# One attention block: TensorE, VectorE and ScalarE in the order of the source from the first head's steps to the last

## The chip, the cores and the metric

The kernel runs on one core of a Trainium2 chip. The metric is device time in microseconds (us) of one execution. Three runs of the kernel before took 638.62, 634.58 and 634.19 us: a median of 634.58 us. The profile comes from one more execution, which took 633.2 us.

## The reference

The kernel computes one residual block with two groups of attention heads that share one input projection. 16 learned rows stand ahead of the 1024 rows of `x`, so L = 1040.

```
h = RMSNorm(x);  proj = h @ w_in         # 1024 -> q, k, v, forget logits, gates, latents
8 FoX heads (width 64):  softmax(q k^T / 8 + sum of log f, causal) v
8 MLA heads (64 + 32 rotary): q and k, v from RMS-normed latents;
                         softmax(q k^T / sqrt(96), a key counts up to the end of the query's chunk of 64) v
y = concat(fox * silu(gate), mla * silu(gate)) @ w_out
out = x + RMSNorm(y), without the 16 learned rows
```

## The kernel before, in words

**Parts.** Operands of TensorE are held as a high and a low 16-bit part, so a product is three matmuls (high x high, high x low, low x high). Up to about 145 us the input is normalised and the first projections run. Then come 16 heads, 8 FoX and 8 MLA, and from about 575 us the output projection and the last norm.

**A step.** A head is four steps, and there are 64 of them. `step` (L891) takes a pair of 128-row query tiles, (7,0), (6,1), (5,2) or (4,3), so each step has 1184 columns of scores in all. In a step:

- `scores` (L798, and the mask as a matmul, L801) fill a PSUM tile `sc`. There are two such tiles, used in turn.
- `peaks` takes the two row maxima on VectorE (L808) and makes the bias `nbs` (L810).
- ScalarE takes two exponentials into `pr`: L905 for the short tile, L907 for the long one (elements in all: 1184 per row).
- `older_step` (L879) multiplies the weights of the step three before (LAG = 3) with the values (L834, L836, L837). Its result goes into the PSUM tile of the step *before this one*, and ScalarE copies it out (L889, `ona`). That copy frees the tile, and the next step's scores are written into that tile.
- `evacuate` empties a product's PSUM that is still owed on VectorE; `low` (L827, VectorE, twice) makes the low parts of the previous step's weights, GpSimd a small strip of them (L921), and SP issues one transposing DMA (L924) that brings them as `pT` to SBUF for the values' matmuls two steps later. `high` (L823) casts this step's weights on ScalarE.

**Jobs between the steps.** `run_head` calls `work` after each step. It issues pieces of what later heads need, each in a `product`, of which two PSUM buffers go round; product k+2 therefore waits until product k has been emptied. The jobs: the next FoX head's projection (L973 to L975, emptied by ScalarE L1060, L1061 and VectorE L1066, L1067); gates (tanh L1085, VectorE L1089 or L1092); MLA queries (weights split by L1179 on ScalarE and L1180 on VectorE, matmuls L1187 to L1189, VectorE L1193, split L144 and L147); MLA keys of two heads (L1205 to L1207 in three pieces, ScalarE L1210 twice and VectorE L1214 twice for each piece); early pieces of the output projection (L1272 to L1274, ScalarE L1291, a DMA to `y_d` L1292). After every second head `pair_end` transposes the outputs (L863, a product too), multiplies by the gate (L865) and splits. Squares of the output weights (L1128), their sum (L1136) and their splitting (L151) are put at given steps.

**What sets the order.** A scheduler places the instructions of every engine by priorities and a cost model of its own; it may hold one back or bring it ahead of what stands earlier in the source. Each engine then runs its list in that order. SP and GpSimd have their own lists.

Of the kernel before, what the change touches and what calls it, by code (L numbers as in the profile page):

```python
# [15 lines left out]
AF = mybir.ActivationFunctionType  # L16
# [32 lines left out]
def hybrid_kernel(ctx, tc, x, meta, norm_pre, norm_post, w_in, b_f, q_norm, w_uq, kv_norm, w_ukv, w_out,  # L49
# [3 lines left out]
    V, A, G, T, SY = nc.vector, nc.scalar, nc.gpsimd, nc.tensor, nc.sync  # L53

    def pool(name, bufs=1, space=None, side=None):
        kw = {}
        if space is not None:
            kw["space"] = space
        if side is not None:
            kw["side"] = side  # L60
        st = ExitStack()
        return st.enter_context(tc.tile_pool(name=name, bufs=bufs, **kw)), st
# [36 lines left out]
    def column(name):  # L99

        col[name] = t = const.tile([P, 1], F32, name=name)
        return t
# [64 lines left out]
    def mul(eng, name, a, b, c=None, op=ALU.mult):  # L167

        t = column(name)
        eng.tensor_scalar(t, a, b, c, ALU.mult, *(() if c is None else (op,)))  # L170
        return t
# [498 lines left out]
    def mla_factors():  # L670


        suk, isuk, suq, isuq, skr = (col[n] for n in ("suk", "isuk", "suq", "isuq", "skr"))
        sqm = mul(G, "sqm", suq, 0.5, CAP, ALU.min)
        skn = mul(G, "skn", suk, 0.125, CAP, ALU.min)
        smin = column("smin")
        G.tensor_scalar(smin, skn, skr, None, ALU.min)
        sm = mul(G, "sm", sqm, smin)
        cmk = mul(G, "cmk", skn, isuk, 1.0 / LATK)
        ism, iskn, iskr = (column(n) for n in ("ism", "iskn", "iskr"))  # L680
        for dst, src in ((ism, sm), (iskn, skn), (iskr, skr)):
            V.reciprocal(dst, src)
        rqs, rq0 = column("rqs"), mul(G, "rq0", sm, isuq, 1.0 / LATQ)
        G.tensor_scalar(rqs[0:64], rq0[0:64], iskn[0:64], None, ALU.mult)
        G.tensor_scalar(rqs[64:P], rq0[64:P], iskr[64:P], None, ALU.mult)
        gqs = const.tile([P, 2], F32, name="gqs")
        G.tensor_scalar(gqs, gq, suq, None, ALU.mult)
        gkvs = mul(G, "gkvs", gkv, suk)
        return ism, cmk, rqs, gqs, gkvs
# [9 lines left out]
    def step_psum(name):  # L699

        return ps_s.tile([P, 1536], F32, name=name, tag="sc")
# [61 lines left out]
    def evacuate():  # L763
        while evacs:
            evacs.popleft()()
# [6 lines left out]
    def product(name):  # L772
        evacuate()
        return ps_g.tile([P, 512], F32, name=name, tag="g")
# [8 lines left out]
    def places(ia, ib):  # L783

        wa, wb = NM + P * (ia + 1), NM + P * (ib + 1)
        a0 = AVW + (wb if (AVW + wa) % 512 < P else 0)
        b0 = AVW + (wa if a0 == AVW else 0)
        assert (a0 + wa - 1) % 512 >= P - 1 and (b0 + wb - 1) % 512 >= P - 1
        return (a0, wa), (b0, wb)

    def scores(i, passes, mask, mask_w, sc, c0, w):

        o = c0
        while o < c0 + w:
            o1 = min(c0 + w, (o // 512 + 1) * 512)
            last = o1 == c0 + w
            for q, (sta, mov) in enumerate(passes):
                T.matmul(sc[:, o:o1], sta[:, i * P : (i + 1) * P], mov[:, o - c0 : o1 - c0],  # L798
                         start=q == 0, stop=q == len(passes) - 1 and not last)
            o = o1  # L800
        T.matmul(sc[:, o - mask_w : o], ident16, mask, start=False, stop=True)  # L801
        return sc[:, c0:o]

    def peaks(parts, inv):

        nb = at.tile([P, 2], F32, name="nb", tag="nb", bufs=4)
        for k, part in enumerate(parts):
            V.tensor_reduce(nb[:, k : k + 1], part, AX.X, ALU.max, negate=True)  # L808
        nbs = at.tile([P, 2], F32, name="nbs", tag="nbs", bufs=4)
        V.tensor_scalar(nbs, nb, inv, LN_PSCALE, ALU.mult, ALU.add)  # L810
        return nbs[:, 0:1], nbs[:, 1:2]
# [6 lines left out]
    def high(i, pr, ph):  # L818
        W = NM + P * (i + 1)
        if i == 0:  # L820
            V.tensor_copy(ph[:, 112 : 112 + W], pr)
        else:
            A.copy(ph[:, 112 : 112 + W], pr)  # L823

    def low(i, pr, ph, lo):
        W = NM + P * (i + 1)
        V.tensor_tensor(lo, pr[:, NM:W], ph[:, P : P + W - NM], ALU.subtract)  # L827

    def weighted(av, i, hi, lo, vh):

        n = i + 1
        for j in range(n + 1):
            vl, v1 = Vt[:, j, vh, 0:HD], Vt[:, j, vh, HD : 2 * HD + 1]
            T.matmul(av, hi[:, j, :], v1, start=j == 0, stop=False)  # L834
            if j > 0:
                T.matmul(av, lo[:, j - 1, :], v1, start=False, stop=False)  # L836
            T.matmul(av[:, 0:HD], hi[:, j, :], vl, start=False, stop=j == n)  # L837
# [41 lines left out]
    def older_step(n, ps):  # L879

        old = steps.get(n - LAG)
        if old is None:
            return
        (ia, ib), pT = old["t"], old["pT"]
        vh, ona, after = old["rest"]
        av = ps[:, 0 : 2 * (HD + 1)].rearrange("p (i d) -> p i d", i=2)
        weighted(av[:, 1], ia, pT, pT[:, B0 + ib + 2 :, :], vh)
        weighted(av[:, 0], ib, pT[:, B0:, :], pT[:, ia + 2 :, :], vh)
        A.copy(ona[:, ib : ia + 1 : ia - ib, :], av)  # L889

    def step(first):  # L891

        now[0] += 1
        n = now[0]
        if first is not None:
            (ia, ib), passes, mask, mask_w, inv = first[0:5]
            last, psc[0] = psc[0], step_psum("sc")
            ps = psc[0]
            (a0, wa), (b0, wb) = places(ia, ib)
            sc = [scores(i, passes, mask, mask_w, ps, c0, w) for i, c0, w in ((ia, a0, wa), (ib, b0, wb))]  # L900
            nbs = peaks(sc, inv)
            pr = last_pr[0] = at.tile([P, wa + wb], F32, name="pr", tag="pr", bufs=2)
            prs = pr[:, 0:wa], pr[:, wa : wa + wb]

            A.activation(prs[1], sc[1], AF.Exp, bias=nbs[1], scale=inv)  # L905
            older_step(n, last)
            A.activation(prs[0], sc[0], AF.Exp, bias=nbs[0], scale=inv)  # L907
            ph = phs[n % NPH]
            la, lb = (B0 + ib + 2) * P, (ia + 2) * P
            los = ph[:, la : la + (ia + 1) * P], ph[:, lb : lb + (ib + 1) * P]  # L910
            steps[n] = dict(t=(ia, ib), pr=prs, prw=pr, ph=ph, phs=(ph, ph[:, B0 * P :]), los=los, rest=first[5:])
        else:
            older_step(n, product("av"))
        evacuate()
        prev = steps.get(n - 1)
        if prev is not None:
            for i, p, h, l in zip(prev["t"], prev["pr"], prev["phs"], prev["los"]):
                low(i, p, h, l)
            ph, n1 = prev["ph"].rearrange("p (b k) -> p b k", k=P), prev["prw"].rearrange("p (b k) -> p b k", k=NM)
            w0 = 1 + 8 * (prev["t"][0] + 1)  # L920
            G.tensor_tensor(ph[:, 0 : B0 + 1 : B0, 96:112], n1[:, 0 : w0 + 1 : w0, :],  # L921
                            ph[:, 0 : B0 + 1 : B0, 112:128], ALU.subtract)
            prev["pT"] = at.tile([P, NBLK * P], F16, name="pT", tag="pT", bufs=3).rearrange("p (b k) -> p b k", k=P)
            SY.dma_start_transpose(prev["pT"], prev["ph"])  # L924
        if first is not None:
            for i, p, h in zip((ia, ib), prs, steps[n]["phs"]):
                high(i, p, h)
        for fn in agenda.pop(n, ()):
            fn()
        old = steps.pop(n - LAG, None)  # L930
        if old is not None:
            (ia, ib), after = old["t"], old["rest"][-1]
            if after is not None:
                after(ia, ib)
# [283 lines left out]
        return [(0.8, gen(c0, n), None) for c0, n in CHUNKS]  # L1218

    ism, cmk, rqs, gqs, gkvs = mla_factors()  # L1220
    wkr = []

    def load_wk():
# [124 lines left out]
    for h in range(H):  # L1348
# [28 lines left out]
        last = (lambda o=onat, p=4 + p4: pair_end(o, p)) if hh else None  # L1377
        run_head(H + h, h, hh, ((QH, KH), (QL, KH), (QH, KL)), blk, 64, ism, onat, last, tiles_end if h == H - 1 else None)


    tl, tl_st = pool("tl", side="left")
    ctx.enter_context(tl_st)
# [66 lines left out]
    for t in order[:2]:  # L1449
        load_late(t)  # L1450
    step(None)
    A.activation(warm, last_pr[0][:, 0:1], AF.Sqrt)
    for t in order[:3]:
        load_rows(t)
    chains.popleft()()
    products(order[0], 0, 7)
    step(None)
    chains.popleft()()
    for k, t in enumerate(order):
# [50 lines left out]
```

## Time and profile before

| | |
|---|---|
| median of three runs | 634.58 us |
| the profiled execution | 633.2 us |
| its span, first to last instruction | 631.0 us |
| around the span | 2.2 us |
| TensorE busy | 559.9 us, 89% |
| VectorE busy | 455.5 us, 72% |
| ScalarE busy | 419.4 us, 66% |
| mean granted TensorE clock | 0.975 |

"Busy" counts time in which at least one instruction of the engine runs. An idle row of an engine matters only where the engine is late for something that sets the end. A granted clock of 1.00 is 2.4 GHz, of 0.50 is 1.2 GHz. Step n is counted from 0, head h has steps 4h to 4h+3; FoX heads are 0 to 7, MLA heads 8 to 15. By the starts of their scores the heads 0 to 14 take 31.2, 32.2, 31.6, 33.3, 30.0, 26.5, 34.7, 30.1 us (FoX) and 21.0, 22.4, 21.1, 25.2, 21.2, 26.7, 18.7 us (MLA).

### The profile page before, as it was taken

What the parts mean: (1) busy time and instruction counts of PE and PEld (TensorE: products, weight loads), DVE (VectorE), ACT (ScalarE), POOL (GpSimd) and SP (SyncE); (2) the same over time, 40 slices, a digit from 0 to 9 for tenths busy, and PEclk for the clock granted to TensorE, in tenths of its full rate; (3) what the DMA queues carried; (4) which work ended last, traced back from release to release, by engine and by line L of the source; (5) the groups of instructions that cost most, each with busy time, mean ns of one, the idle gap of its engine ahead of it and who ended that gap; (6) DMA issues with size and microseconds to landing.
All of it is one profiled execution on the core that took longest, in us unless ns stands there. A gap on an engine that the chain in (4) does not pass through costs nothing.

```text
span 631.0 us, 12856 instructions
## 1 busy us (share of the span) xinstructions
PE 559.9 (89%) x4914; PEld 339.2 (54%) x4914; DVE 455.5 (72%) x889; ACT 419.4 (66%) x756; POOL 197.5 (31%) x283
## 2 busy tenths in 40 slices
PE   2999799989898988999988897887989979989994
PEld 1445354546465655756666454554656656655442
DVE  3778876576767775767676667779777867777667
ACT  5788868456867776656657748578777767677322
POOL 2223333372224242324331322123322212331242
PEclk9999899999899999999999998999989989999998
DMA  8858768165687896696968588977978777698953
GB/s 286 213 133 222 152 175 211 33 179 162 123 179 144 195 192 120 123 194 141 166 127 177 100 199 175 192 148 131 167 168 163 142 156 160 129 189 191 302 180 120
DMA packets 269533, 105.11 MB, mean 167 GB/s; under 512 B 234832, under 2 KB 257360, under 8 KB 269472
## 3 DMA queue, kind: packets, MB, share of 16 engines
q1 hardware_dynamic: 269472, 104.30, 74.2%
q8 instruction: 38, 0.62, 0.4%
q14 instruction: 23, 0.19, 0.1%
HBM read 48.38 MB, written 13.96 MB: 99 GB/s over the span
## 4 chain that ended last, share of the span: by engine, by line
DVE 19%; PE 18%; ACT 12%; issue 7%; DMA 7%; SPq 2%; POOL 0%; DVEq 0%; ACTq 0%; POOLq 0%
DVE nb L808 7%; ACT pr L907 4%; DMA pT<-ph 4%; ACT ph L823 4%; DVE ph L827 3%; PE sc L798 2%; PE psf L1274 2%; PE psf L1272 2%; PE psf L1273 2%; DVE nbs L810 1%; DMA wqr<-in_w_uq 1%; SPq L924 1%; PE psg L973 1%; PE psg L975 1%; PE psg L974 1%
## 5 line engine op out<-in xcount | busy, mean ns | idle before, releaser
L827 DVE TENSOR_TENSOR ph<-pr,ph 128x512 f16<-128x512 f32 (+7 forms) x128 | 99.4, 782 | 67.7 <-ACT ph L823 66.7
L921 POOL TENSOR_TENSOR ph<-pr,ph 128x32 f16<-128x32 f32 x64 | 53.1, 830 | 228.1 <-ACT ph L823 106.7
L808 DVE TENSOR_REDUCE nb<-sc 128x1 f32<-128x1040 f32 (+7 forms) x128 | 93.2, 766 | 6.9 <-PE sc L801 6.3
L798 PE MATMUL sc<-st,st 128*128 128x256 f16 (+5 forms) x496 | 76.8, 293 | 8.5 <-ACT ona L889 7.3
L823 ACT CAST ph<-pr 128x784 f16<-128x784 f32 (+6 forms) x112 | 78.0, 740 | 0.2
L798 PEld LDWEIGHTS <-st 128*128 128x128 f16 x640 | 56.8, 99 | 37.5 <-issue 9.0
L834 PE MATMUL sc<-Vt,pT 128*128 128x65 f16 x671 | 64.7, 195 | 11.4 <-ACT pr L907 8.8
L837 PEld LDWEIGHTS <-pT 128*128 128x128 f16 x704 | 63.0, 99 | 11.6 <-issue 10.8
L837 PE MATMUL sc<-Vt,pT 128*128 128x64 f16 x671 | 66.5, 194 | 0.0
L834 PEld LDWEIGHTS <-pT 128*128 128x128 f16 x704 | 62.5, 98 | 7.2 <-DMA pT<-ph 4.8
L836 PE MATMUL sc<-Vt,pT 128*128 128x65 f16 x549 | 60.8, 195 | 0.0
L836 PEld LDWEIGHTS <-pT 128*128 128x128 f16 x576 | 53.6, 98 | 0.0
L973 PEld LDWEIGHTS <-wp 128*128 128x128 f16 x320 | 31.4, 98 | 34.3 <-DVE st L1067 12.2
L905 ACT ACTIVATE pr<-sc,nbs,fox_inv 128x144 f32<-128x144 f32 (+3 forms) x32 | 20.1, 629 | 43.3 <-DVE nbs L810 37.5
L974 PEld LDWEIGHTS <-wp 128*128 128x128 f16 x320 | 31.5, 98 | 25.5 <-issue 4.8
L975 PEld LDWEIGHTS <-wp 128*128 128x128 f16 x320 | 31.4, 98 | 25.0 <-issue 0.8
L973 PE MATMUL psq<-xAh,wp 128*128 128x264 f16 x128 | 35.6, 278 | 5.0 <-DVE st L1067 3.1
L905 ACT ACTIVATE pr<-sc,nbs,ism 128x144 f32<-128x144 f32 (+3 forms) x32 | 20.2, 631 | 23.1 <-DVE nbs L810 20.4
L975 PE MATMUL psq<-xAh,wp 128*128 128x264 f16 x128 | 35.5, 277 | 0.0
L974 PE MATMUL psq<-xAl,wp 128*128 128x264 f16 x128 | 35.5, 277 | 0.0
L907 ACT ACTIVATE pr<-sc,nbs,ism 128x1040 f32<-128x1040 f32 (+3 forms) x32 | 33.7, 1052 | 0.0
L907 ACT ACTIVATE pr<-sc,nbs,fox_inv 128x1040 f32<-128x1040 f32 (+3 forms) x32 | 33.6, 1051 | 0.0
(373 smaller groups left out, 1540.2 us busy)
## 6 DMA issues: line engine op xcount, KB each, us to landing
wr<-in_w_in SPq DMA_DIRECT2D x20, 512.0 KB
wr<-in_w_in SPq DMA_DIRECT2D x26, 256.0 KB
wor<-in_w_out SPq DMA_DIRECT2D x8, 512.0 KB
xr<-in_x SPq DMA_DIRECT2D x8, 512.0 KB
xt<-in_x SPq DMA_DIRECT2D x7, 512.0 KB
y_d<-ys SPq DMA_DIRECT2D x12, 256.0 KB
y<-y_d SPq DMA_DIRECT2D x6, 512.0 KB
out<-y SPq DMA_DIRECT2D x5, 512.0 KB
```

Of the source, the lines that this page charges most:

```text
L798: T.matmul(sc[:, o:o1], sta[:, i * P : (i + 1) * P], mov[:, o - c0 : o1 - c0], start=q == 0, stop=q == len(passes) - 1 and not last)
L808: V.tensor_reduce(nb[:, k : k + 1], part, AX.X, ALU.max, negate=True)
L823: A.copy(ph[:, 112 : 112 + W], pr)
L827: V.tensor_tensor(lo, pr[:, NM:W], ph[:, P : P + W - NM], ALU.subtract)
L834: T.matmul(av, hi[:, j, :], v1, start=j == 0, stop=False)
L836: T.matmul(av, lo[:, j - 1, :], v1, start=False, stop=False)
L837: T.matmul(av[:, 0:HD], hi[:, j, :], vl, start=False, stop=j == n)
L907: A.activation(prs[0], sc[0], AF.Exp, bias=nbs[0], scale=inv)
L921: G.tensor_tensor(ph[:, 0 : B0 + 1 : B0, 96:112], n1[:, 0 : w0 + 1 : w0, :], ph[:, 0 : B0 + 1 : B0, 112:128], ALU.subtract)
L973: T.matmul(ps[:, 0:n], hi[:, c, :], xT(0, c, c0, n), start=c == 0, stop=False)
L974: T.matmul(ps[:, 0:n], hi[:, c, :], xT(1, c, c0, n), start=False, stop=False)
L975: T.matmul(ps[:, 0:n], lo[:, c, :], xT(0, c, c0, n), start=False, stop=c == NC - 1)
```

## The change

From the start of the jobs of the MLA set-up (L1220, after the first FoX head's projection has been issued and before the first step) to the end of the last MLA head, TensorE, VectorE and ScalarE get their instructions in the order in which the source issues them. The scheduler still orders SP and GpSimd there, and everything before and after. In `step`, the long exponential is also issued ahead of `older_step`, where it stood behind it. Lines behind L1220 move by 3, behind L1383 by 4.

```diff
@@ -903,8 +903,8 @@
             A.activation(prs[1], sc[1], AF.Exp, bias=nbs[1], scale=inv)
+            A.activation(prs[0], sc[0], AF.Exp, bias=nbs[0], scale=inv)
             older_step(n, last)
-            A.activation(prs[0], sc[0], AF.Exp, bias=nbs[0], scale=inv)
             ph = phs[n % NPH]
@@ -1218,6 +1218,9 @@
     ism, cmk, rqs, gqs, gkvs = mla_factors()
+
+    in_order = ExitStack()
+    in_order.enter_context(tc.manual_schedule(engines={mybir.EngineType.PE, mybir.EngineType.DVE, mybir.EngineType.Activation}))
     wkr = []
@@ -1377,6 +1380,7 @@
         run_head(H + h, h, hh, ((QH, KH), (QL, KH), (QH, KL)), blk, 64, ism, onat, last, tiles_end if h == H - 1 else None)
+    in_order.close()
```

ScalarE in step 48, the first of MLA head 12 (`ona` is the copy that frees a scores tile, `pr` the exponentials, `ph` the casts). Before:

```order
L823 CAST ph_1699<-pr 128x528
L823 CAST ph_1699<-pr 128x656
L889 COPY ona<-sc 128x2x65
L905 ACTIVATE pr<-sc,nbs,ism 128x144
L907 ACTIVATE pr<-sc,nbs,ism 128x1040
```

Now:

```order
L823 CAST ph_1699<-pr 128x656
L823 CAST ph_1699<-pr 128x528
L905 ACTIVATE pr<-sc,nbs,ism 128x144
L906 ACTIVATE pr<-sc,nbs,ism 128x1040
L889 COPY ona<-sc 128x2x65
L823 CAST ph_1700<-pr 128x1040
```

The copy stood ahead of both exponentials of its step, as in most MLA steps of before, and now stands behind them, as in all.

TensorE in head 13, whose jobs hold three pieces of keys (`psk`), the transposes `pso` of the pair before, and the next queries (`psq`). Before, the last piece of keys came a whole step after the second; where it stood:

```order
L1207 LDWEIGHTS wk_l
L1207 MATMUL psk<-ck_1715,wk_l 128x346
L798 LDWEIGHTS st_1694
L798 MATMUL sc<-st_1696,st_1694 128x256
...
L836 MATMUL sc<-Vt,pT 128x65
L837 LDWEIGHTS pT
L837 MATMUL sc<-Vt,pT 128x64
L798 LDWEIGHTS st_1694
L798 MATMUL sc<-st_1696,st_1694 128x368
L863 MATMUL pso<-ident,onatm 128x128 x4
L798 LDWEIGHTS st_1695
```

Now:

```order
L1207 LDWEIGHTS wk_l
L1207 MATMUL psk<-ck_1715,wk_l 128x346
L863 MATMUL pso<-ident,onatm 128x128 x4
L1205 LDWEIGHTS wk_h
L1205 MATMUL psk<-ck_1715,wk_h 128x348
L1206 LDWEIGHTS wk_h
L1206 MATMUL psk<-ck_1716,wk_h 128x348
L1207 LDWEIGHTS wk_l
L1207 MATMUL psk<-ck_1715,wk_l 128x348
L1187 LDWEIGHTS wqh
L1187 MATMUL psq<-cqh,wqh 128x512
```

A step's scores and values (45 matmuls) stood between the second piece and the transposes; now three pieces of keys, transposes and queries follow one another without other work between them, and the next step's scores come behind all of them.

VectorE in the same place of head 11 (`wql`, `kl`, `st` are the jobs' low parts, `nb` the row maxima of the next step). Now:

```order
L1180 SCALAR_TENSOR_TENSOR wql<-wqr,gqs,wqh 128x128 x2
L1214 SCALAR_TENSOR_TENSOR kl_4696<-psk,cmk,kh_4695 64x346
L1214 SCALAR_TENSOR_TENSOR st_1697<-psk,cmk,st_1696 64x346
L1214 SCALAR_TENSOR_TENSOR kl_4696<-psk,cmk,kh_4695 64x346
L1214 SCALAR_TENSOR_TENSOR st_1697<-psk,cmk,st_1696 64x346
L865 SCALAR_TENSOR_TENSOR og<-pso,gatem 128x512
L1214 SCALAR_TENSOR_TENSOR kl_4696<-psk,cmk,kh_4695 64x348
L1214 SCALAR_TENSOR_TENSOR st_1697<-psk,cmk,st_1696 64x348
L808 TENSOR_REDUCE nb<-sc 128x1 x2
```

All of it stands ahead of the next step's maxima; before, one of those maxima (L808) stood ahead of the first L1214.

## Rows read from the trace of the kernel before

**Rows 1.** The page: busy time, share of the span and instructions of each engine.
```profile
PE 559.9 (89%) x4914; PEld 339.2 (54%) x4914; DVE 455.5 (72%) x889; ACT 419.4 (66%) x756; POOL 197.5 (31%) x283
```

**Rows 2.** Windows: head 0, heads 1–6, head 7, heads 8–14, most of 15.
```profile
core 0: us, PE busy (x) PEld busy (x) DVE busy (x) ACT busy (x) POOL busy (x), PEclk, DMA share, GB/s
145.40:176.60 31.20, 28.39 (x197) 16.41 (x195) 23.31 (x41) 22.17 (x36) 7.26 (x13) 0.95 0.69 138
176.60:364.90 188.30, 175.40 (x1705) 113.97 (x1704) 130.20 (x209) 126.77 (x209) 60.82 (x75) 0.99 0.77 154
364.90:395.10 30.20, 25.19 (x240) 15.16 (x238) 21.38 (x40) 20.00 (x37) 8.04 (x8) 0.94 0.85 189
395.10:551.40 156.30, 139.34 (x1568) 89.79 (x1567) 120.22 (x208) 111.02 (x191) 41.92 (x48) 0.97 0.80 156
551.40:575.00 23.60, 20.88 (x240) 13.24 (x238) 19.30 (x37) 19.05 (x32) 6.64 (x7) 1.00 0.87 164
```

**Rows 3.** Waits, 150 to 395: engine, line, releaser, total us, times, longest.
```profile
PEld L973 <- DVE st L1067: 11.2, 7, 2.3
```

**Rows 4.** Waits, 395 to 571 (MLA steps).
```profile
PE sc L798 <- ACT ona L889: 8.9, 5, 2.7
PE sc L834 <- ACT pr L907: 6.7, 9, 1.5
```

**Rows 5.** Timeline of step 55 and the start of 56: start, us, engine, line.
```profile
529.71 1.00 PE L798 MATMUL sc<-st,st 128*128 128x256 f16 x6
...
531.25 0.19 PE L801 MATMUL sc<-blk,ident 128*128 128x64 bf16 x1
...
531.48 1.46 DVE L808 TENSOR_REDUCE nb<-sc 128x1 f32<-128x656 f32 x2 [0.76 <-PE sc L801]
...
532.42 0.27 ACT L889 COPY ona<-sc 128x130 f32<-128x130 f32 x1
...
532.74 0.38 PE L798 MATMUL sc<-kh,st 128*128 128x256 f16 x2
...
533.30 0.79 ACT L905 ACTIVATE pr<-sc,nbs,ism 128x528 f32<-128x528 f32 x1 [0.61 <-DVE nbs L810]
...
533.99 0.89 ACT L907 ACTIVATE pr<-sc,nbs,ism 128x656 f32<-128x656 f32 x1
```

**Rows 6.** Windows: head 4, head 6, scores and values of step 55, step 48.
```profile
273.81:303.82 30.01, 29.76 (x289) 19.28 (x288) 21.07 (x34) 19.59 (x30) 9.87 (x12) 1.00 0.87 166
330.29:364.96 34.67, 30.24 (x289) 19.30 (x288) 22.37 (x36) 23.93 (x41) 9.14 (x12) 1.00 0.67 139
529.71:532.22 2.51, 2.51 (x47) 2.02 (x46) 1.75 (x3) 0.56 (x1) 0.00 (x0) 1.00 0.67 175
484.83:491.20 6.37, 6.12 (x63) 3.62 (x61) 4.48 (x10) 4.98 (x8) 0.83 (x1) 1.00 0.68 148
```

**Rows 7.** Window: head 11's first three steps (44 to 46).
```profile
459.64:481.81 22.17, 19.04 (x186) 11.67 (x184) 17.41 (x29) 17.85 (x32) 6.89 (x8) 0.92 0.75 150
```

**Rows 8.** Groups by form, 395 to 551: the jobs' emptying instructions.
```profile
L147 DVE TENSOR_TENSOR st<-qt,st 128x512 f16<-128x512 f32 x7 | 4.9, 694 | 0.0
L1214 DVE SCALAR_TENSOR_TENSOR st<-psk,cmk,st 64x346 f16<-64x346 f32 x8 | 4.6, 577 | 0.1
L865 DVE SCALAR_TENSOR_TENSOR og<-pso,gatem 128x512 f32<-128x512 f32 x4 | 2.8, 690 | 1.5 <-PE pso L863 1.5
L1210 ACT ACTIVATE st<-psk,cmk 64x346 f16<-64x346 f32 x8 | 4.4, 547 | 0.1
L1179 ACT ACTIVATE wqh<-wqr,gqs 128x128 f16<-128x128 f32 x10 | 3.6, 399 | 4.5 <-DMA wqr<-in_w_uq 3.5 <-PE psq L1188 0.8
```

**Rows 9.** ScalarE in head 0: one square, one split.
```profile
147.54 0.72 ACT L1128 ACTIVATE junkw<-wor,inv_g 128x512 bf16<-128x512 f32 x1
...
163.38 1.15 ACT L151 ACTIVATE wp<-wr,bsc 128x1024 f16<-128x1024 f32 x1
```

**Rows 10.** Window at the lower clock, in head 11.
```profile
470.10:473.50 3.40, 3.40 (x11) 1.41 (x10) 2.78 (x6) 2.32 (x5) 1.16 (x1) 0.50 0.31 83
```

## The prediction, made before the changed kernel was run

> **What bounds the kernel now.** I read the page first, then windows by head, then the waits, then the timeline of single steps. TensorE is busy 559.9 of 631.0 us [rows 1], so only its 71 idle us can be won, and a new order can at most move them. The windows say where they lie [rows 2]: 12.9 us in FoX heads 1 to 6 (188.30 less 175.40), 2.8 in head 0, 5.0 in head 7, 17.0 in MLA heads 8 to 14 (156.30 less 139.34). The waits name the causes, and they differ. In the FoX heads the projection's next product waits for VectorE to empty the one two before: 11.2 us at L973, released by L1067 [rows 3]. In the MLA heads the scores wait 8.9 us for the copy L889 that frees their tile, and the values 6.7 us for the long exponential [rows 4].
>
> The timeline shows what the scheduler does with that copy [rows 5]. In step 55 the scores start at 529.71, the copy runs at 532.42, ahead of the step's own exponentials at 533.30, and the next scores start at 532.74, only 3.03 us after the last ones. The two scores tiles are thus filled ahead, and a stretch of jobs later uses up the lead. Seven MLA heads take 156.3 us for 28 steps, 5.58 each, jobs included.
>
> **The change part by part.**
>
> *The loop of a light MLA step.* In source order, with the swap, ScalarE runs both exponentials, then the copy, then the casts. So step n+1's scores can't start before step n's scores, maxima, bias, exponentials and copy have run one after another. From step 55 [rows 5]: scores 529.71 to 531.44, 1.73; to the end of the two maxima at 532.94, 1.50; to the exponentials at 533.30, 0.36; to their end at 534.88, 1.58; copy 0.27, from which I take 0.1, since neighbours on ScalarE overlap by that much (533.99 against 534.09); and 0.05 from the copy's end at 532.69 to the scores at 532.74. Together **5.4 us**. Scores and values are only 2.51 us of TensorE [rows 6], so 2.9 us are free for jobs, and left idle where there are none; this idle time can't be given back to a later step.
>
> *28 MLA steps, heads 8 to 14.* 28 x 5.4 = 151.2. Five steps carry both a query product and an early output product; such a step took 6.37 us with 6.12 busy [rows 6], so 5 x 0.97 = 4.9 more. In the first step of heads 11 and 13 the order rows show three pieces of keys, the transposes and the queries in a row, with two PSUM buffers. The transposes wait until the first piece has been emptied, and that waits on ScalarE behind exponentials and copy (5.4 into the step), a cast (about 1.0, as an exponential of the same width takes), two splits L1179 (0.80) and two copies L1210 (1.09): 8.3. VectorE then has four L1214 (2.31) ahead of the gate product L865 (0.69), and the queries reuse the transposes' buffer, so they start at about 11.3 and take some 0.4 until the next scores may follow: about 11.7 instead of 5.4, twice [rows 8], +12.6. Before, these pieces lay apart by a whole step, and head 11's first three steps took 22.17 us with 3.1 idle [rows 7]; the same three would now be 11.7 + 5.4 + 6.4 = 23.5. In head 9 the pieces of keys and two transposes are spread over three steps; by the same chain of L1210, L1214 and L865 I take 4.1 in all. In heads 10, 12 and 14 VectorE meets a query product's second part, which waits for ScalarE's first, ahead of the previous step's low parts and the next maxima: 0.4 of waiting and one operation of 0.7, like the gate product's 0.69 [rows 8], so 1.1 each, 3.3. Sum 151.2 + 4.9 + 12.6 + 4.1 + 3.3 = 176.1 against 156.3: **+19.8**. Low bound: all chains hidden leaves 156.1, nothing gained or lost. High bound: +28, if head 9's chains are as long as head 11's.
>
> *FoX heads 1 to 6.* There the loop is no limit: head 4 took 30.01 us with TensorE busy 29.76 [rows 6], 7.5 a step. `evacuate` stands right behind the maxima in the source and ahead of the low parts, so L1066 and L1067 now come early, and the 11.2 us at L973 should mostly go. Head 6 shows what such waits cost: 34.67 us, 30.24 busy [rows 6]. Late next are the transposes' gate products (L865), one or two for each second head, behind the maxima: 3 to 4 us stay. I take **-9**; bounds -12.9 (all idle time) and -4.
>
> *Head 0.* Before, its first scores were spread among the projection; now they stand behind it, and ScalarE runs four squares (0.72 each) and splits of 1.15 [rows 9] where the source has them, between step 2's casts and a tanh on which the next product waits: 4 x 0.72 + 2 x 1.15 = 5.2. Its 2.8 idle us cover about half. **+3**; bounds 0 (covered) and +6.
>
> *Head 7.* Gate, query and key products of different kinds follow each other. Each pair of L1210 and pair of L1214 is 1.09 + 1.15 [rows 8]; before, scores lay between the key pieces. Three pieces expose 6.7 at most, and the present 5.0 idle us are partly the same waits. **+3**; bounds -3 and +7.
>
> *Head 15.* Four splits of output weights stand in order ahead of maxima; tail work is outside the ordered part. **+1**; bounds 0 and +3.
>
> *SP and GpSimd.* They stay scheduled. The low parts come about one maxima pair (1.46) later than before, and the transposing DMA behind them. With steps of 5.4 the values need it two steps on, 10.8 us, so I count nothing; if the steps were as short as 3.0 that cover would be gone.
>
> *The clock.* In head 11 the granted clock was 0.50 for 3.40 us [rows 10], 1.2 instead of 2.4 GHz, which costs half of it, 1.7. My sum for the MLA heads holds no such stretch, and the two long waits should bring one each, perhaps less than whole: **+2**; bounds 0 and, by the rival below, +14.
>
> Sum: 19.8 - 9 + 3 + 3 + 1 + 2 = +19.8. The profiled execution took 633.2 us (631.0 span and 2.2 around), so 633.2 + 19.8 = **653.0 us**; the median of the runs shown, 634.58, is 1.4 above that execution, which is within the uncertainty.
>
> **The rivals.**
>
> 1. *Faster: the order wins in both groups.* Place: the MLA steps. If the first L1210 and L1214 of a chain run in the 2.9 us that each light step leaves free, and the loop is shorter because the maxima of the first tile overlap the second tile's scores, 0.7 of 1.5 us a step, the steps come to 4.7 us where light. For it: one row of the timeline groups two maxima, and nothing in the order forbids the first to start early. Against: in step 55 VectorE had been idle 0.76 us when it was released by the last mask matmul (L801), after both tiles. Decides: a mean MLA step under 5.4 us in place of 6.3. Then 28 x 5.3 is 148.4, -8, with FoX -9 and the rest +6: 633.2 - 11 = 622. Chance 0.08.
> 2. *No change.* The loop is as I say, but the chains of products lie beside it. MLA +0 to +6, FoX -9, the rest +6 to +9: 630 to 639, about 636. For it: TensorE has 12 us of slack in 28 loops (151.2 less 139.3). Against: the order rows of head 13 leave nothing between the pieces to hide behind. Chance 0.14.
> 3. *Worse: the clock.* Every light step without a job now idles 2.9 us. If after each of them the clock falls as in head 11, at 1.7 a time, some eight steps cost 14 us: 653 + 12 = 665, up to 670 with late transposes. The Trainium skill (TensorE: Matmul & The Clock Gate, section HAM oscillation — how this bites in real kernels) describes a loop where each wait between bursts of matmuls brought the lower clock back, each burst beginning cold; by that rule this rival would hold. The trace agrees in part: head 11 has such a stretch [rows 10], but waits of up to 2.7 us at the scores [rows 4] lie in heads 8 to 14 too, and their mean clock is 0.97 [rows 2]. Chance 0.10.
> 4. *The order isn't what it says.* The rows of the order exclude it for ScalarE, VectorE and TensorE.
>
> **The numbers.** The forecast, 643 to 662 with its bounds, has 0.68. The range from 637 to 668 leaves out rival 1, part of rival 2 and the end of rival 3: 2 in 10. A measurement of this kernel can tell about 1%, 6.3 us, from no change. Slower than that: the forecast, rival 3 and a little of rival 2, 0.79; within: most of rival 2, 0.13; faster: rival 1, 0.08.
>
> **What would show it.** Right: the starts of MLA scores without jobs 5.2 to 5.6 us apart, each released by L889; a first step of heads 11 and 13 of 11 to 12 us with idle time at the transposes, the third piece of keys and the queries; the wait of L973 for L1067 in FoX heads 1 to 6 under 4 us; head 7 longer than 30.2. Wrong: MLA light steps under 5, or FoX heads 1 to 6 still near 188, or long waits for `pT`.

## The result and the profile after

The changed kernel takes 704.93 us (704.28 to 705.73, four runs); the kernel before, run beside it, 636.6 us. The ratio is 1.1075, 95% interval 1.102 to 1.113: **slower by 10.8%, 68 us, where 653.0 us had been forecast and 637 to 668 given as the range.** The sign was right, the size was short by more than half.

The profiled execution has a span of 704.0 us against 631.0. The page's line of engines:

```profile
PE 584.7 (83%) x4914; PEld 346.4 (49%) x4914; DVE 451.5 (64%) x889; ACT 414.9 (59%) x756; POOL 159.8 (23%) x283
```

VectorE and ScalarE do the same work in about the same time as before, 4 us less each [rows 1]. TensorE issues the same 4914 matmuls but is busy 24.8 us longer, and idle 48.2 us longer (119.3 against 71.1). The 73.0 us of span are these two. Windows by stretch, for head 0, heads 1 to 6, head 7, heads 8 to 14 (they answer to [rows 2]):

```profile
144.27:188.58 44.31, 33.22 (x198) 17.80 (x196) 20.49 (x36) 22.41 (x37) 5.62 (x13) 0.85 0.50 101
188.58:383.78 195.20, 178.89 (x1705) 114.61 (x1704) 128.02 (x210) 117.75 (x194) 41.90 (x75) 0.97 0.68 142
383.78:425.81 42.03, 28.92 (x238) 15.34 (x237) 24.09 (x40) 19.86 (x36) 5.53 (x7) 0.80 0.73 164
425.81:620.54 194.73, 151.42 (x1568) 94.62 (x1567) 119.98 (x214) 112.13 (x198) 30.41 (x48) 0.90 0.64 128
```

| stretch | before | after | moved | forecast | TensorE idle before, after |
|---|---|---|---|---|---|
| head 0 | 31.2 | 44.3 | +13.1 | +3 | 2.8, 11.1 |
| heads 1 to 6 | 188.3 | 195.2 | +6.9 | -9 | 12.9, 16.3 |
| head 7 | 30.1 | 42.0 | +11.9 | +3 | 5.0, 13.1 |
| heads 8 to 14 | 156.4 | 194.7 | +38.4 | +19.8 | 17.0, 43.3 |
| head 15 and tail | 79.6 | 83.4 | +3.8 | +1 | |
| ahead of head 0 | 145.4 | 144.3 | -1.1 | 0 | |

A light MLA step does what the forecast said. Timeline of step 55 (scores from 590.51) and the start of step 56; the answer to [rows 5]:

```profile
592.05 0.19 PE L801 MATMUL sc<-blk,ident 128*128 128x64 bf16 x1
592.28 1.46 DVE L808 TENSOR_REDUCE nb<-sc 128x1 f32<-128x656 f32 x2 [0.40 <-PE sc L801]
...
594.12 0.79 ACT L905 ACTIVATE pr<-sc,nbs,ism 128x528 f32<-128x528 f32 x1 [2.37 <-DVE nbs L810]
594.81 0.89 ACT L906 ACTIVATE pr<-sc,nbs,ism 128x656 f32<-128x656 f32 x1
595.59 0.27 ACT L889 COPY ona<-sc 128x130 f32<-128x130 f32 x1
595.91 0.58 PE L798 MATMUL sc<-kh,st 128*128 128x256 f16 x2 [2.73 <-ACT ona L889]
```

Maxima, bias, exponentials, copy and scores follow one another, and 590.51 to 595.91 is 5.40 us; ten of the 28 steps take 5.39 or 5.40, and behind each of them the copy L889 is what releases the next scores.

The first step of head 11 (from 509.91) shows the row of products. Timeline of ScalarE, VectorE and TensorE:

```profile
515.14 1.07 ACT L823 CAST ph<-pr 128x1040 f16<-128x1040 f32 x1
516.10 0.70 ACT L1179 ACTIVATE wqh<-wqr,gqs 128x128 f16<-128x128 f32 x2
516.69 0.54 ACT L1210 ACTIVATE kh<-psk,cmk 64x346 f16<-64x346 f32 x1
...
518.41 0.58 DVE L1214 SCALAR_TENSOR_TENSOR st<-psk,cmk,st 64x346 f16<-64x346 f32 x1
...
520.26 0.69 DVE L865 SCALAR_TENSOR_TENSOR og<-pso,gatem 128x512 f32<-128x512 f32 x1
...
519.14 1.08 PE L863 MATMUL pso<-ident,onatm 128*128 128x128 f32 x4 [4.89 <-DVE st L1214]
...
521.09 0.63 PE L1187 MATMUL psq<-cqh,wqh 128*128 128x512 f16 x1
...
523.56 1.33 PE L798 MATMUL sc<-st,st 128*128 128x256 f16 x9
```

The queries start 11.2 us into the step, where the working had 11.3. The next scores come at 13.65, not 11.7: 0.4 us had been counted for the six query matmuls, and they took 2.5, at half the clock.

In the FoX heads a wait appears that the working had priced in head 0 alone. Waits of heads 1 to 6 (engine, line, releaser, us, times, longest):

```profile
DVE wp L152 <- ACT wp L151: 29.6, 13, 5.4
...
PE psg L973 <- DVE st L1067: 5.6, 5, 3.0
...
PEld L973 <- DVE st L1067: 1.2, 3, 0.6
```

The wait of L973's weight load for L1067, the row that the forecast went by, has fallen to 1.2, from 11.2 [rows 3], there over a somewhat longer stretch; the wait of L973's matmuls for the same line has not (5.6). And VectorE now waits 29.6 us at L152, the low part of the weights of the next job, for its high part L151. The timeline of steps 22 and 23 in head 5, VectorE, then ScalarE, shows what hangs on it:

```profile
346.07 1.47 DVE L152 SCALAR_TENSOR_TENSOR wp<-wr,bsc,wp 128x1024 f16<-128x1024 f32 x1 [3.01 <-ACT wp L151]
347.58 0.49 DVE L1066 SCALAR_TENSOR_TENSOR st<-psq,fox_c,st 64x264 f16<-64x264 f32 x1
348.08 0.50 DVE L1067 SCALAR_TENSOR_TENSOR st<-psq,fox_c,st 64x264 f16<-64x264 f32 x1
348.61 1.46 DVE L808 TENSOR_REDUCE nb<-sc 128x1 f32<-128x656 f32 x2
...
344.89 1.15 ACT L151 ACTIVATE wp<-wr,bsc 128x1024 f16<-128x1024 f32 x1
350.44 0.79 ACT L905 ACTIVATE pr<-sc,nbs,fox_inv 128x528 f32<-128x528 f32 x1 [4.40 <-DVE nbs L810]
```

ScalarE comes to L151 only behind step 22's casts and emptyings; VectorE waits for it with the next step's maxima behind; ScalarE then has nothing to do for 4.40 us, since it waits for the bias of those maxima. The scores of step 24 then wait 3.3 us for the copy behind these exponentials. The two engines wait for each other by turns; VectorE does so at L152 13 times in these 24 steps.

The lower clock, in head 0's projection, in head 11's row of products, and in step 56's scores:

```profile
150.80:158.80 8.00, 8.00 (x34) 3.62 (x33) 1.92 (x4) 3.27 (x4) 0.25 (x1) 0.75 0.00 0
...
519.10:523.50 4.40, 4.34 (x13) 2.06 (x14) 2.49 (x5) 1.71 (x3) 1.15 (x1) 0.51 0.51 114
...
595.91:598.91 3.00, 3.00 (x20) 1.73 (x20) 0.00 (x0) 1.11 (x2) 0.24 (x1) 0.56 0.86 159
```

Each stands behind an idle stretch of TensorE: 4.3, 4.9 and 2.7 us.

### The profile page after: what moved, and what is told of

Read it like the earlier page. It is cut to its first block, busy times and chain, and to the rows that moved or that the text cites. A ratio compares the mean times of both kernels' runs of the same rounds, so it can differ in the third digit from the quotient of the medians.

```text
span 704.0 us, 12827 instructions
## 1 busy us (share of the span) xinstructions
PE 584.7 (83%) x4914; PEld 346.4 (49%) x4914; DVE 451.5 (64%) x889; ACT 414.9 (59%) x756; POOL 159.8 (23%) x283
## 4 chain that ended last, share of the span: by engine, by line
PE 41%; DVE 24%; ACT 21%; issue 7%; DMA 5%; SPq 1%; POOL 0%; ACTq 0%; DVEq 0%
PE sc L798 8%; DVE nb L808 8%; ACT pr L906 6%; ACT ph L823 4%; PE psg L973 2%; PE psg L975 2%; PE psg L974 2%; DVE wp L152 2%; PE psq L975 2%; PE psq L973 2%; PE psq L974 2%; DMA wr<-in_w_in 2%; ACT wp L151 2%; PE psf L1277 2%; PE psf L1275 2%
## 5 line engine op out<-in xcount | busy, mean ns | idle before, releaser
L808 DVE TENSOR_REDUCE nb<-sc 128x1 f32<-128x1040 f32 (+7 forms) x128 | 92.8, 766 | 58.3 <-PE sc L801 57.7
L798 PE MATMUL sc<-st,st 128*128 128x256 f16 (+4 forms) x496 | 78.2, 301 | 21.6 <-ACT ona L889 13.5
L798 PEld LDWEIGHTS <-st 128*128 128x128 f16 x640 | 59.6, 103 | 72.0 <-issue 24.3
L827 DVE TENSOR_TENSOR ph<-pr,ph 128x1024 f16<-128x1024 f32 (+7 forms) x128 | 91.2, 754 | 0.4
L921 POOL TENSOR_TENSOR ph<-pr,ph 128x32 f16<-128x32 f32 x64 | 17.5, 273 | 287.8 <-ACT ph L823 169.3
L823 ACT CAST ph<-pr 128x1040 f16<-128x1040 f32 (+6 forms) x112 | 78.9, 753 | 0.1
L834 PE MATMUL sc<-Vt,pT 128*128 128x65 f16 x671 | 65.5, 196 | 2.2 <-DMA pT<-ph 2.2
L834 PEld LDWEIGHTS <-pT 128*128 128x128 f16 x704 | 62.6, 99 | 5.7 <-DMA pT<-ph 3.9
L973 PEld LDWEIGHTS <-wp 128*128 128x128 f16 x320 | 32.2, 101 | 41.3 <-DVE kl L1214 7.3
L152 DVE SCALAR_TENSOR_TENSOR wp<-wr,bsc,wp 128x1024 f16<-128x1024 f32 x21 | 28.4, 1358 | 36.8 <-ACT wp L151 36.8
L974 PEld LDWEIGHTS <-wp 128*128 128x128 f16 x320 | 32.2, 101 | 33.3 <-issue 14.3
L975 PEld LDWEIGHTS <-wp 128*128 128x128 f16 x320 | 32.2, 101 | 29.7 <-issue 5.4
L973 PE MATMUL psq<-xAh,wp 128*128 128x264 f16 x128 | 35.3, 276 | 1.9 <-DVE og L865 1.2
L973 PE MATMUL psg<-xBh,wp 128*128 128x512 f16 x64 | 25.9, 405 | 11.7 <-DVE kl L1214 7.0
```

Source lines behind the costliest of these rows:

```text
L152: V.scalar_tensor_tensor(lo, raw, scale, hi, ALU.mult, ALU.subtract)
L973: T.matmul(ps[:, 0:n], hi[:, c, :], xT(0, c, c0, n), start=c == 0, stop=False)
L974: T.matmul(ps[:, 0:n], hi[:, c, :], xT(1, c, c0, n), start=False, stop=False)
L975: T.matmul(ps[:, 0:n], lo[:, c, :], xT(0, c, c0, n), start=False, stop=c == NC - 1)
```

## The experiments

The theory: instructions that empty a job's product, split its weights or copy a scores tile now stand on ScalarE and VectorE behind work that they don't need; TensorE waits, and its clock falls in the waits. All the kernels ran beside the kernel before. The table gives the median, the ratio with its interval to the runs of before taken beside it (their means lie between 633 and 637), and the stretches of the one profiled execution in us.

| kernel | us | ratio | head 0 | 1 to 6 | 7 | 8 to 14 |
|---|---|---|---|---|---|---|
| before | 636 | | 31.2 | 188.3 | 30.1 | 156.4 |
| the change | 704.9 | 1.108 (1.102 to 1.113) | 44.3 | 195.2 | 42.0 | 194.7 |
| e1_noswap | 698.6 | 1.096 (1.088 to 1.105) | 44.0 | 196.5 | 40.8 | 184.7 |
| e3_pe | 656.8 | 1.031 (1.023 to 1.038) | 39.4 | 190.6 | 34.2 | 165.2 |
| e4_act | 699.7 | 1.098 (1.092 to 1.104) | 35.8 | 203.5 | 35.4 | 194.7 |
| e5_dve | 646.4 | 1.014 (1.009 to 1.020) | 23.5 | 190.9 | 31.3 | 170.8 |
| g2_pe_dve | 667.9 | 1.055 (1.049 to 1.062) | 37.6 | 184.4 | 43.2 | 172.6 |
| f1_copyfirst | 690.3 | 1.084 (1.075 to 1.094) | 44.4 | 194.5 | 39.9 | 179.5 |
| f2_latecasts | 680.5 | 1.069 (1.060 to 1.078) | 41.4 | 184.2 | 38.8 | 187.4 |
| f3_keys | 705.3 | 1.108 (1.098 to 1.118) | 44.1 | 195.0 | 42.0 | 193.8 |
| i1_inside | 687.4 | 1.086 (1.080 to 1.093) | 36.5 | 188.3 | 40.4 | 190.3 |
| f4_three | 662.6 | 1.041 (1.032 to 1.050) | 41.3 | 182.4 | 36.9 | 172.8 |
| i2_four | 667.3 | 1.050 (1.045 to 1.054) | 38.5 | 184.6 | 42.0 | 173.2 |
| h1_warm | 702.9 | 1.111 (1.104 to 1.117) | 46.7 | 193.8 | 39.6 | 191.2 |
| g1_fox16 | 636.1 | 1.002 (0.998 to 1.006) | 30.3 | 189.5 | 32.4 | 157.8 |
| j2_dve36 | 632.5 | 0.994 (0.992 to 0.996) | 31.2 | 188.2 | 29.5 | 158.8 |
| j3_dve06 | 633.5 | 0.997 (0.994 to 1.000) | 23.5 | 196.4 | 29.4 | 157.0 |

**The swap undone.**

```diff
             A.activation(prs[1], sc[1], AF.Exp, bias=nbs[1], scale=inv)
-            A.activation(prs[0], sc[0], AF.Exp, bias=nbs[0], scale=inv)
             older_step(n, last)
+            A.activation(prs[0], sc[0], AF.Exp, bias=nbs[0], scale=inv)
```

> The change without its swap: ScalarE has short exponential, copy of the older step, long exponential, in order. Theory (the time is lost where job products stand in a row and their emptying instructions are behind the step's own work on ScalarE and VectorE; the clock falls in those waits): only the MLA loop gets shorter, by about the long exponential (5.39 to some 4.5 us a light step), so 5 to 18 us less: 687 to 700. Rival A (the copy behind both exponentials is the main cost): most of the 70 us comes back, under 660.

6 us less by the medians. In the profiled execution heads 8 to 14 are 10.0 faster, and the rest gives about 1 of it back. Of the 68 us the swap is a small part.

**One engine at a time.** Each edit changes only the set of engines in order: `{PE}`, `{Activation}`, `{DVE}`, and `{PE, DVE}`; the swap stays in all four.

```diff
-    in_order.enter_context(tc.manual_schedule(engines={mybir.EngineType.PE, mybir.EngineType.DVE, mybir.EngineType.Activation}))
+    in_order.enter_context(tc.manual_schedule(engines={mybir.EngineType.Activation}))
```

> Only TensorE in source order in the same stretch (its list is that of the change), ScalarE and VectorE scheduled. Theory (the lists of ScalarE and VectorE hold the emptying instructions back): most comes back, 635 to 660, with short waits at the products. Rival B (TensorE's own order is the cause, since scores and values no longer stand between products): 680 or more, the long waits at the keys, the transposes and the query products still there.

> Only ScalarE in source order with the swap, TensorE and VectorE scheduled. Theory: ScalarE alone costs the loop (copy behind exponentials) and the emptying behind exponentials and casts: 655 to 685. Rival B: near before, 630 to 645.

> Only VectorE in source order, TensorE and ScalarE scheduled. Theory: VectorE alone costs where maxima stand behind weight parts and low parts that wait for ScalarE: 640 to 665, less than ScalarE's part. Rival B: near before, 630 to 645, or a little faster, since the FoX products are emptied earlier.

> TensorE and VectorE in source order, ScalarE scheduled; the only difference to the change is ScalarE's order. Theory (ScalarE's list costs most, the other two little beyond it): 650 to 668, MLA heads 8 to 14 below 175. Rival (each engine's order costs what it cost alone, and they would add): above 665, MLA 180 or more.

TensorE's order costs 20 us, VectorE's 10, the two together 32. ScalarE's alone, with the swap, costs 63, more than the 20 to 50 that I had expected of it. The windows of e4_act over heads 1 to 6 and 8 to 14:

```profile
179.51:383.05 203.54, 179.31 (x1705) 114.18 (x1704) 136.35 (x212) 118.04 (x195) 56.48 (x76) 0.98 0.69 140
418.43:613.11 194.68, 153.66 (x1583) 95.29 (x1582) 123.74 (x212) 110.72 (x196) 45.06 (x47) 0.93 0.64 128
```

The MLA heads take 194.7 us with ScalarE alone in order, the same total as with all three, but not by the same waits. TensorE's largest in these heads, in e4_act, then in the change:

```profile
PE sc L834 <- ACT pr L906: 23.7, 18, 3.5
...
PE sc L798 <- ACT ona L889: 17.3, 12, 2.7
```

There the values wait for the exponentials, here the scores wait for the copy, so that the totals agree is no proof of one mechanism. With ScalarE alone left to the scheduler, heads 1 to 6 and 8 to 14 of g2_pe_dve:

```profile
182.67:367.07 184.40, 175.37 (x1706) 113.01 (x1704) 127.36 (x210) 121.22 (x198) 43.38 (x74) 0.99 0.76 154
410.31:582.95 172.64, 144.26 (x1568) 91.60 (x1567) 118.75 (x212) 112.99 (x194) 31.76 (x48) 0.92 0.72 143
```

The FoX heads then win 3.9 us against before. So in both groups ScalarE's list weighs most: 37 of the 68 us come back when it is left to the scheduler. The costs don't add, since 63 alone and 32 without it make 95. In heads 0 and 7 it isn't so: without it head 0 keeps 6.4 of its 13.1 us, and head 7 takes 43.2.

**What stands in the wrong place on ScalarE.** Four moves, each with the order kept. The copy ahead of the exponentials:

```diff
+            older_step(n, last)
             A.activation(prs[1], sc[1], AF.Exp, bias=nbs[1], scale=inv)
             A.activation(prs[0], sc[0], AF.Exp, bias=nbs[0], scale=inv)
-            older_step(n, last)
```

> The change with the older step's values and their copy issued ahead of both exponentials. Theory (ScalarE's list is what holds the MLA loop: the copy stands behind work it doesn't need): scores no longer wait for exponentials, light MLA steps fall from 5.39 to 3.5 to 4.5 us, MLA heads 8 to 14 from 194.7 to some 165 to 175, total 675 to 690. Rival A (the step is bound by something else, weights transposed too late or VectorE): light steps stay over 5 and the total over 695.

The casts of step n at the start of step n+1, ahead of its exponentials:

```diff
         n = now[0]
+        while owed:
+            oa, ob, oprs, ophs = owed.pop()
+            for i, p, h in zip((oa, ob), oprs, ophs):
+                high(i, p, h)
...
         if first is not None:
-            for i, p, h in zip((ia, ib), prs, steps[n]["phs"]):
-                high(i, p, h)
+            owed.append((ia, ib, prs, steps[n]["phs"]))
```

> The change with the casts of a step's weights issued at the start of the next step, so that the emptying of job products stands ahead of them on ScalarE, and the casts in the time in which ScalarE waits for the bias. Theory: products are emptied 1.1 to 1.3 us earlier in each step with jobs; long waits at keys, queries and projections get shorter, total 680 to 698. Rival A: the low parts come later and the values wait for their transposes: 705 or more.

Keys apart, and weights split behind the maxima:

```diff
-        js = in_turn("kkkqoqo" if ks else "qoqo", q=qs, k=ks, o=os)
+        js = in_turn("kqkoqok" if ks else "qoqo", q=qs, k=ks, o=os)
```

> The change with the three pieces of keys apart, a query product or an early output between them, in heads 9, 11 and 13. Theory (pieces in a row on two buffers wait for their emptying): the first steps of heads 11 and 13 fall from 13.6 and 13.1 to 7 to 9 us and head 9 by 3 to 5; total 690 to 697. Rival: the chain behind the step's exponentials and casts sets it, not the row of pieces, and the later steps get what the first lose: 702 to 706.

```diff
-            if k < 2 and o.loaded is not None and o.parts and (now[0] > o.loaded + 1 or j is jobs[0]):
+            if k < 2 and o.loaded is not None and o.parts and (ahead and now[0] > o.loaded + 1 or j is jobs[0]):
...
             nbs = peaks(sc, inv)
+            prepare(True)
```

> The change with the splitting of weights for the next jobs (L151 and L152, L1179 and L1180) issued behind a step's maxima and ahead of its exponentials, instead of behind its casts. Theory (in FoX heads VectorE stands at L152 for ScalarE's L151, and the next maxima behind it: 15 times, 36.8 us in the change): FoX heads 1 to 6 fall from 195 to 183 to 188, head 7 by 2 to 5, total 688 to 698. Rival (these waits lie beside TensorE's projections): 702 or more.

The copy ahead of the exponentials brings five of the ten light steps down to 3.0 and 3.8 us; four stay at 5.1 to 5.3 and one rises to 6.7. The MLA heads come down by 15, less than expected; the first steps of heads 11 and 13 grow, from 13.6 and 13.1 to 15.1 and 14.9. The late casts bring 24 us, 11 of them in heads 1 to 6, which fits the emptying of products and the splits having stood behind the casts; which of the two it was isn't shown. The keys apart bring nothing: the first steps of heads 11 and 13 fall to 11.0 and 10.3, and the first of heads 12 and 14 rise to 10.6 and 9.8, so the loss moves with the pieces and isn't that of the row alone. The split weights bring 17.5 us: 6.9 in heads 1 to 6, 7.8 in head 0, which I had not expected, and only 1.6 in head 7. Their wait in heads 1 to 6 with that edit:

```profile
DVE wp L152 <- ACT wp L151: 13.6, 3, 6.0
```

Three such waits are left of 13, and 13.6 of 29.6 us.

> The change with all three: copy ahead of the exponentials, late casts, keys apart. Theory: the gains add to a good part, 645 to 675, still above the kernel before, because the FoX heads keep most of their waits. Rival: they overlap, over 680.

> The change with copy ahead of the exponentials, late casts, keys apart, and weights split behind the maxima. Theory (the cost is where a few ScalarE instructions stand in the source, not that the order is fixed): the four gains add mostly, 662.6 less the 8 to 17 of the split weights, 645 to 655, MLA heads under 173. Rival (a fixed order loses by itself, whatever stands where): 658 or more.

Copy, casts and keys together bring 42 us back, and the heads 1 to 6 at 182.4 are 5.9 faster than before. With the split weights added it is 667.3 instead of 662.6: the gains don't add, head 7 is back at 42.0. None of the sets that were run with the order kept came within 26 us of the kernel before, and what makes these 26 us stays open.

**The clock.** Matmuls that nobody reads, put ahead of six products in heads 0, 7, 9, 11 and 13 (478 in all, written to columns of the scores tile that are not in use):

```diff
+    KEEP = {(3, 1): 40, (29, 0): 70, (30, 2): 120, (36, 2): 100, (44, 2): 76, (52, 2): 72}
...
+    def keep_on(k):
+        for _ in range(KEEP.get((now[0] - 2, k), 0)):
+            T.matmul(psc[0][:, 1440:1536], ident16, blk96, start=True, stop=True)
...
     def product(name):
         evacuate()
+        pcount[:] = (pcount[0], pcount[1] + 1) if pcount[0] == now[0] else (now[0], 0)
+        keep_on(pcount[1])
```

> The change, with 478 small matmuls (128x96, results used by nobody) put ahead of six products at which TensorE waits longest (heads 0, 7, 9, 11, 13), so that it is busy while it waits. Theory (part of the 25 us is that TensorE works at 1.2 GHz behind those waits, on the path): the lower clock behind them goes, 690 to 698. Rival (the lower clock lies beside other waits): 703 to 708.

2 us less by the medians, short of the theory; by the ratios, 1.111 and 1.108 with intervals that overlap, no gain is shown. Windows over head 7 and heads 8 to 14:

```profile
384.77:424.42 39.65, 33.43 (x428) 23.73 (x427) 24.09 (x40) 19.86 (x36) 5.54 (x7) 0.96 0.82 171
424.42:615.58 191.16, 155.34 (x1816) 103.93 (x1816) 120.01 (x214) 112.43 (x198) 30.42 (x48) 0.96 0.64 130
```

The granted clock rises from 0.80 to 0.96 and from 0.90 to 0.96, and these heads get 2.4 and 3.6 us faster; head 0 gets 2.4 slower, since the added matmuls there wait 5.9 us for the exponentials that read the tile. So the clock's part that lies on the path in heads 7 to 14 is about 6 us by this one trace, at the five of the places that lie there. It doesn't reach the other places with a lower clock (the scores of steps 40, 48 and 56, for instance), and the added matmuls take time themselves, so the whole of it stays open; TensorE is busy 24.8 us longer in all.

**Source order for a part only.** In g1_fox16 the three engines are in order in heads 1 to 6, with three of the moves. In the last two VectorE alone is, without the swap; the edit of j2_dve36:

```diff
+    in_order = ExitStack()
...
         pr_i, hh = divmod(h, 2)
+        if h == 3:
+            in_order.enter_context(tc.manual_schedule(engines={mybir.EngineType.DVE}))
...
+    in_order.close()
     xat_st.close()
```

> Source order for FoX heads 1 to 6 alone, with the copy ahead of the exponentials, late casts and weights split behind the maxima there; the scheduler orders the rest, as before the change. Theory: these heads take 175 to 182 instead of 188.3 and the rest is as before: 622 to 632. Rival (what is won there comes back at the ends of the stretch): 633 to 642.

> Only VectorE in source order, for FoX heads 3 to 6 alone, without the swap; the rest scheduled. Theory (VectorE's early emptying of projections helps where ScalarE may run ahead): these heads took 117.6 us with VectorE in order from head 0 on against 124.5 before, so 626 to 633. Rival (what it wins comes back in head 7): 634 to 640.

> Only VectorE in source order, for FoX heads 0 to 6, without the swap; the rest scheduled. Theory: heads 0 to 6 took 214.4 us in such an order against 219.5, so 627 to 634. Rival: head 7 gives it back, 634 to 640.

The heads 1 to 6 of g1_fox16, with the three engines in order and three of the moves, took 189.5 us, not 175 to 182, and the time is that of before. VectorE alone in order in heads 3 to 6 gives 632.5 us, ratio 0.994 (0.992 to 0.996, twelve runs): faster than both kernels, by 3 us, the best of three partial orders. Its profiled execution doesn't show where (span 631.1 against 631.0; heads 3 and 5 are 3.5 and 2.0 faster, heads 4 and 6 1.9 and 3.1 slower), so that stays open.

## Why the prediction was wrong

- *The loop of 5.4 us*: right to a hundredth, 5.39 to 5.40, released by L889 as said.
- *28 MLA steps, +19.8; measured +38.4.* The working gives about 21.6, 25.7, 23.7, 28.9, 23.7, 28.9 and 23.7 us for heads 8 to 14; they took 24.5, 32.7, 26.8, 30.8, 24.9, 30.3 and 24.6. The working of the row of keys held to 0.1 us until the queries started, 11.2 us into the first steps of heads 11 and 13, and then left out the queries themselves (2.5 and 1.9 us). The five steps with a query and an output product were put at 6.37; two took 6.38, and the first steps of heads 10, 12 and 14 took 9.6, 7.9 and 7.7, where scores ran at the lower clock (3.0 us instead of 1.73 in step 56). The largest miss is head 9: the working took its keys as partly hidden, and its first step alone took 11.4, with 6.3 us of TensorE waiting at the second piece.
- *Heads 1 to 6, -9; measured +6.9. This is the step that failed outright.* The sum let the 11.2 us at L973 go and put 3 to 4 of L865 in their place. The 11.2 were the row of a weight load [rows 3]. L973's matmuls waited 8.4 us for L1067 in these heads, and 5.6 of that stayed. TensorE's waits in heads 1 to 6, two lines before, three now:

```profile
PE psg L973 <- DVE st L1067: 6.0, 4, 2.2
PE psq L973 <- DVE st L1067: 2.4, 2, 1.5
...
PE psg L973 <- DVE st L1067: 5.6, 5, 3.0
PE sc L798 <- ACT ona L889: 5.3, 2, 3.3
PE psq L973 <- DVE ge L1092: 2.8, 1, 2.8
```

  The working asked what is late next and named the gate product L865, which costs 1.2 us here; it was the splitting of weights, L151 and L152, which the source issues behind the casts and ahead of the next maxima. It was in the rows for head 0 alone [rows 9], and was not followed through the other heads. Moving it gave 6.9 us there, moving the casts 11.0. The loss lies in heads 2, 4 and 5 (+7.5, +2.5, +4.5), and heads 1, 3 and 6 win 7.5. Head 2 has the second set of squares L1128: VectorE's L152 waits 5.4 us for an L151 behind them, and the gate L1092, for which TensorE waits 2.8 us, stands behind that L152. TensorE is also busy 3.5 us longer in the six heads.
- *Head 0, +3; measured +13.1.* TensorE waits 4.8 us in step 3 for the gate behind squares and splits, as said. The working also said that the first scores now stand behind the projection, but gave that no price: they wait 4.3 us for the DMA of the decays (`cum_d`, L1054), and they and the next eight us of projection run partly at 1.2 GHz. TensorE is busy 4.8 us longer in this head, and 2.0 us more go to a wait for L1067.
- *Head 7, +3; measured +11.9.* The bound of +7 counted the key pieces' own emptying, 6.7 us. In the trace, step 29's first query product waits 5.0 us for the split of its weights on ScalarE (L1179), and step 30's keys stand on ScalarE behind copy, casts, two L1179 and an L151, and the gate product waits 6.96 us for them:

```profile
410.82 0.70 ACT L1179 ACTIVATE wqh<-wqr,gqs 128x128 f16<-128x128 f32 x2
411.42 1.14 ACT L151 ACTIVATE wp<-wr,bsc 128x1024 f16<-128x1024 f32 x1
412.45 0.54 ACT L1210 ACTIVATE st<-psk,cmk 64x346 f16<-64x346 f32 x1
...
415.59 0.61 PE L973 MATMUL psg<-xBh,wp 128*128 128x512 f16 x1 [6.96 <-DVE kl L1214]
```

  The experiments don't settle head 7: TensorE's order alone costs it 4.1, ScalarE's 5.3, VectorE's 1.2, TensorE's and VectorE's together 13.1.
- *The clock, +2.* TensorE is busy 24.8 us longer with the same matmuls. Rival 3 had the mechanism, the clock falling in the waits, with a price of 14 and a chance of 0.10. In heads 8 to 14 six of the 28 steps have scores of 3.0 us or more, together some 9 us above the 1.73 of the working; two of them, steps 48 and 56, follow a light step without a product, where the rival put it, and the other four follow other waits. Steps 48 and 46 carry the same products; the windows of their scores:

```profile
540.73:543.96 3.23, 3.23 (x18) 2.00 (x18) 0.00 (x0) 1.11 (x2) 0.24 (x1) 0.50 0.87 162
...
528.95:530.68 1.73, 1.73 (x20) 1.28 (x20) 0.02 (x1) 1.73 (x4) 1.16 (x1) 1.00 0.21 41
```

  The steps took 7.93 and 6.38 us, so there the lower clock is on the path. But the rival's 665 to 670 us was far short of 705 too. The Trainium skill (TensorE: Matmul & The Clock Gate, section HAM oscillation — how this bites in real kernels) describes a loop in which each wait for DMA between bursts of matmuls brings the lower clock back. The trace agrees in part: the six steps, behind waits of 2.1 to 6.3 us, do so, and steps 42, 50 and 58, behind waits of 1.4 us, don't.
- *SP and the transposes, nothing*: right; by the page of the profile the first weight loads of the values (L834) wait 3.9 us for `pT` in all, 4.8 before.
- *Rivals 1 and 2* are excluded: MLA steps mean 6.95 us, far above 5.4.

Most of the misses have one form. I followed each chain on the engine that does the work and added it to the step, but not what stands behind it on the next engine: an L152 that waits for L151 holds maxima, these hold a bias, exponentials and a copy, that copy holds the next scores. In a fixed order such a wait is passed on to all that stands behind it.

## What to carry to other kernels

An order that is fixed on one engine is judged by what stands behind each instruction that waits: list, for every such wait, the next instruction on that engine and who waits for it. Fix one engine at a time: here ScalarE, 66% busy before, by itself cost 63 us, and of the 68 of all three 37 came back without it; VectorE alone, in four heads, won 0.6%. Moving single groups of instructions inside a fixed order gave up to 24 us each. Three of these moves together gave about their sum, the fourth on top lost 5, so a sum of such moves has to be run, not added up.

## What the runs showed of the hardware that I had not expected

The same idle time had not the same sequel. In the kernel before, TensorE stood 2.65 us (404.11 to 406.76) ahead of step 34's scores, and they ran at full clock; in the changed one it stood 2.73 us ahead of step 56's, and they ran at 0.56. The window of the first, in the kernel before:

```profile
406.70:409.70 3.00, 2.94 (x48) 2.25 (x48) 1.41 (x3) 2.89 (x6) 0.22 (x1) 1.00 0.89 204
```

What tells the two apart was not tried. And TensorE kept busy with small matmuls raised the granted clock of heads 8 to 14 from 0.90 to 0.96, but the time fell by only 3.6 of 194.7 us: a higher mean clock was worth little here, in this one trace.
